# Page scores of a paged-attention decode step: five dimension steps in three runs instead of five single steps

## Chip, cores and metric

The kernel runs on one core of a Trainium2 chip. The metric is the device time of one execution in microseconds (us), lower is better. An execution consists of one program for five engines: TensorE (PE, matmuls and, as PEld, its weight loads), VectorE (DVE), ScalarE (ACT), GpSimd (POOL) and SyncE (SP, which only issues transfers here).

## The reference

One layer of a hybrid decoder is computed for a prompt of 1024 tokens and, with the same weights, for 8 sequences of 4 new tokens. The change concerns only the second attention branch of the 8 sequences. Each of them has 64 pages of 128 past tokens in a paged cache; each past token has a latent of 256 dimensions and a rotary key of 64. All 8 heads share these keys, and the latent is the value too:

```python
def one_seq(args):
    ql, qr, pt, c_new, r_new = args
    c_past = cache_ckv[pt].reshape(-1, KV_LORA)
    r_past = cache_kr[pt].reshape(-1, MLA_ROPE)
    s_past = jnp.einsum('thc,kc->htk', ql, c_past) + jnp.einsum('thr,kr->htk', qr, r_past)
    ...
    sc = jnp.concatenate([s_past.astype(jnp.float32) * scale, s_new], axis=-1)
    p = jax.nn.softmax(sc, axis=-1).astype(c_new.dtype)
    n_past = c_past.shape[0]
    return (jnp.einsum('htk,kc->thc', p[..., :n_past], c_past)
            + jnp.einsum('htk,kc->thc', p[..., n_past:], c_new))
```

So a score is a sum over 320 dimensions, in any order of the dimensions. The rest of the layer (projections of x, retention, prompt attention, down projections, output, norms) is not touched.

## The kernel before

The kernel goes through its stages in order: latents of all tokens, queries of the 8 sequences, page attention, retention of four heads, prompt attention of eight heads, down projections, output. In the early stages two streams are written out together: a main stream and a fill, the fill being the input projections `gate_tiles` whose results go to DRAM. Both are Python generators that yield an assumed cost. `beside(main, total, fill, budget)` draws from the fill whenever the fill's share of its budget lies behind the main stream's share of its total. For page attention this is `beside(page_attention(), 505, fill, 321)`: for each unit of cost that the main stream yields, 321/505 units of fill follow. One step of the fill (`mac` in `gemm`, lines 268 to 270) is three matmuls of 128x128 weights with 352 columns and yields 0.441. A third of a projection is eight such steps, ended by an evacuation on ACT (L441) and a store issued by ACT. The weights of the next projection are loaded by SP (L248) into two halves, turned into a high part on ACT (L249) and a low part on DVE (L200).

`page_attention` treats the 8 sequences in four groups `g` of two, and the 64 pages in four parts `jj`: 16 units. Before the first unit of a group, `new_tokens` scores the new tokens. A unit is `past_keys(g, jj, st)`:

- POOL gathers the rope keys (`rraw`, two rooms) and the latents (`craw`, four rooms: this unit's and the next one's) of both sequences with indirect DMAs (L631, L632).
- Five dimension steps, the rope's (j = 8) first, then j = 0, 2, 4, 6. A step turns 64 dimensions of both sequences with four DVE transposes (L691) into a room `kt`. There are two such rooms. Then it issues 16 matmuls (L695) on 32x32 tiles of PE's array, which add up in the four PSUM banks of `sc`. A matmul of 32-bit floats stands as two in the trace, so a step has 32 there.
- Softmax: ACT copies half of the sums out (L706), DVE adds the other half and takes the maximum (L707), ACT takes the exponentials (L711).
- PE transposes the probabilities (L720), ACT and DVE copy them out (L721), PE weights the latents with them on four column tiles (L726), DVE adds the result up (L728). L726 is the last reader of the unit's `craw` rooms.

A unit yields 5.0 behind the gathers, 2.5 between steps, 12.0 behind the softmax, 1.0 behind each half of the transposes and 1.0 at its end.

Within these streams, the order on each engine's queue is made by a planner. It takes the instructions as emitted unless it expects one not to be ready, in which case it puts a later one ahead. It also adds the waits and hands out the rooms: a room is given to the next tile once all readers of the last one are through.

## Time and profile before

| | us |
|---|---|
| median of 3 runs (2117.35 to 2122.88) | 2119.05 |
| span of the profiled execution | 2129.5 |
| PE busy in the span | 2079.5 |
| DVE, ACT, POOL busy | 1237.4, 692.8, 305.4 |
| page attention, about 185 to 725 us of the span: PE busy | 534.27 of 540 |
| the same stretch: DVE busy | 303.64 |

Busy time of PE is a union of matmuls that overlap in a pipeline and whose ends are modelled, so an engine that is busy all the time can still start matmuls closer together or farther apart; starts tell more than ends. In rows of the trace, "x32" is the number of instructions merged into one row, and what stands in brackets is the idle time before it and what ended it.

### The profile page before, as it was taken

How to read it: one execution, taken by the hardware profiler on the slowest of the kernel's cores; microseconds unless marked ns; L12 is line 12 of the kernel's file. 1: busy time of each engine (PE TensorE's matmuls, PEld its weight loads, DVE VectorE, ACT ScalarE, POOL GpSimd, SP SyncE). 2: the span in 40 equal slices, each digit the busy share in tenths (PEclk: the TensorE clock that was granted, in tenths of full speed). 3: DMA queues.
4: the chain of work that ended last, by engine and by line, in shares of the span. 5: the costliest groups of instructions: out<-in, count | busy, mean ns of one | idle time of the engine just before them, and what ended most of it. 6: DMA issues, size and time to landing. Idle time of an engine off the chain costs nothing. (4 is left out here: it accounts for less than half of the span.)

```text
span 2129.5 us, 38253 instructions
## 1 busy us (share of the span) xinstructions
PE 2079.5 (98%) x15122; PEld 1792.7 (84%) x15122; DVE 1237.4 (58%) x2699; ACT 692.8 (33%) x1455; POOL 305.4 (14%) x517
## 2 busy tenths in 40 slices
PE   8999999999999999999999999999999999999998
PEld 7898777777777897888878786788888999999976
DVE  6524555465655357667676663877777465454443
ACT  6312222433333222222222221454556232232221
POOL 2210110111110022222222120122211000000000
PEclk9999999999999999999999999999999999999999
DMA  7576656566565332554634746210112565236642
GB/s 211 129 241 211 234 186 237 187 244 216 211 228 178 111 94 51 175 163 120 204 67 151 191 134 221 64 49 18 38 52 92 187 217 173 89 122 132 172 153 91
DMA packets 387188, 321.90 MB, mean 151 GB/s; under 512 B 197984, under 2 KB 332320, under 8 KB 382912
## 3 DMA queue, kind: packets, MB, share of 16 engines
q1 hardware_dynamic: 290816, 205.86, 33.0%
q0 software_dynamic: 9216, 83.89, 10.5%
q10 hardware_dynamic: 86976, 29.70, 5.2%
q8 instruction: 119, 1.95, 0.4%
q14 instruction: 61, 0.50, 0.1%
HBM read 246.69 MB, written 72.69 MB: 150 GB/s over the span
## 5 line engine op out<-in xcount | busy, mean ns | idle before, releaser
L268 PE MATMUL mm<-xh,wh 128*128 128x352 f32 x1344 | 456.5, 340 | 4.8 <-ACT gev L441 3.2
L270 PE MATMUL mm<-xh,wl 128*128 128x352 f32 x1344 | 437.0, 325 | 2.1 <-DVE wl L200 2.1
L269 PE MATMUL mm<-xl,wh 128*128 128x352 f32 x1344 | 436.7, 325 | 0.0
L268 PEld LDWEIGHTS mm<-xh,wh 128*128 128x128 f32 x1344 | 253.7, 189 | 88.5 <-issue 76.8
L270 PEld LDWEIGHTS mm<-xh,wl 128*128 128x128 f32 x1344 | 254.6, 189 | 2.9 <-DVE wl L200 2.4
L269 PEld LDWEIGHTS mm<-xl,wh 128*128 128x128 f32 x1344 | 254.7, 189 | 2.5 <-issue 1.3
L691 DVE STREAM_TRANSPOSE kt<-craw 128x512 f32<-128x512 f32 x256 | 161.3, 681 | 108.8 <-PE sc L695 75.4
L200 DVE TENSOR_TENSOR wl<-wr,wh 128x512 fp32r<-128x512 f32 (+2 forms) x203 | 136.9, 686 | 98.7 <-ACT wh L249 69.1
L249 ACT CAST wh<-wr 128x512 fp32r<-128x512 f32 x150 | 89.8, 617 | 196.5 <-PE mm L269 169.8
L441 ACT ACTIVATE gev<-mm 128x352 f32<-128x352 f32 x120 | 55.5, 462 | 230.4 <-PE mm L270 221.8
L268 PE MATMUL mm<-mh,wh 128*128 128x352 f32 x384 | 124.8, 325 | 2.2 <-ACT mh L1210 0.8
L269 PE MATMUL mm<-ml,wh 128*128 128x352 f32 x384 | 124.7, 325 | 0.8 <-DVE ml L200 0.6
L270 PE MATMUL mm<-gh,wl 128*128 128x352 f32 x384 | 124.3, 324 | 0.0
L268 PE MATMUL mm<-gh,wh 128*128 128x352 f32 x384 | 124.3, 324 | 0.0
L270 PE MATMUL mm<-mh,wl 128*128 128x352 f32 x384 | 124.2, 324 | 0.0
L269 PE MATMUL mm<-gl,wh 128*128 128x352 f32 x384 | 124.1, 323 | 0.0
L268 PE MATMUL mm<-wv,xh 128*128 128x512 f32 x256 | 101.7, 397 | 0.0
L270 PE MATMUL mm<-wv,xl 128*128 128x512 f32 x256 | 100.9, 394 | 0.0
L269 PE MATMUL mm<-wv,xh 128*128 128x512 f32 x256 | 100.8, 394 | 0.0
L695 PE MATMUL sc<-kt,q 32*32 32x512 f32 x2560 | 91.2, 600 | 0.0
L268 PEld LDWEIGHTS mm<-mh,wh 128*128 128x128 f32 x384 | 72.4, 189 | 3.2 <-ACT gh L1210 1.2
L269 PEld LDWEIGHTS mm<-ml,wh 128*128 128x128 f32 x384 | 72.3, 188 | 1.6 <-DVE ml L200 1.4
(416 smaller groups left out, 4292.3 us busy)
## 6 DMA issues: line engine op xcount, KB each, us to landing
wr<-in_w_in_dram SPq DMA_DIRECT2D x144, 256.0 KB, 3.5
st<-in_state_ret_dram SPq DMA_DIRECT2D x32, 512.0 KB, 5.7
out_ret_sample_dram<-st SPq DMA_DIRECT2D x32, 512.0 KB, 3.1
gt<-gev ACTq DMA_DIRECT2D x48, 176.0 KB, 2.1
gl<-go SPq DMA_DIRECT2D x16, 528.0 KB, 5.1
rg<-gt SPq DMA_DIRECT2D x16, 528.0 KB, 4.2
gate<-ga SPq DMA_DIRECT2D x16, 528.0 KB, 3.6
wvS<-in_w_in_dram SPq DMA_DIRECT2D x32, 256.0 KB, 4.6
```

The lines of the kernel that those rows point to most:

```text
L200: dve.tensor_tensor(out=out, in0=src, in1=b32(hi), op=ALU.subtract)
L249: hi_by[0](hi, raw)
L268: pe.matmul(out, wh, xh, start=first, stop=False)
L269: pe.matmul(out, wh, xl, start=False, stop=False)
L270: pe.matmul(out, wl, xh, start=False, stop=last)
L441: a = act.activation(t, ps, func)
L691: dve.transpose(kt[:, 2 * i + s].rearrange("p (n r) -> p n r", r=32), src)
L695: pe.matmul(sc[32 * v:32 * v + 32, q, :], Q["q4"][qs_, j + v // 2, 2 * (g % 2) + v % 2, :], kt[qs_, v, :], start=n == 0, stop=n == NJ // 2 ...
```

## The change

The five steps of a unit are done in three runs: (j = 0 and 8), (4 and 2), (6). In a run all transposes are issued first, into both rooms, those of the second step of the run ahead of those of the first; then the matmuls of both steps follow with no yield between them. The accumulation starts at j = 0 and stops at j = 6. The yields of the unit are dealt anew: 1.0 behind the gathers (5.0 before), 8.4 behind the first run and 4.6 behind the second (four times 2.5 before), 13.0 behind the softmax (12.0 before). Their sum over a unit is 30.0 as before, and the arguments of `beside` stay.

```diff
-        yield 5.0
+        yield 1.0
         sc = psg.tile([P, 4, 512], F32, tag="sc", name="sc", bufs=1)
-        steps = [8, *range(0, 8, 2)]
-        for n, j in enumerate(steps):
-            kt = ring("kt")
-            for i in range(2):
-                for s in range(2):
-                    src = keys[s][:, :, 32 * (j + i):32 * (j + i) + 32] if j < 8 else rope[s][:, :, 32 * i:32 * i + 32]
-                    dve.transpose(kt[:, 2 * i + s].rearrange("p (n r) -> p n r", r=32), src)
-            for q in range(4):
-                qs_ = slice(32 * q, 32 * q + 32)
-                for v in range(4):
-                    pe.matmul(sc[32 * v:32 * v + 32, q, :], Q["q4"][qs_, j + v // 2, 2 * (g % 2) + v % 2, :], kt[qs_, v, :], start=n == 0,
-                              stop=n == NJ // 2 - 1, tile_position=(32 * q, 32 * v), skip_group_check=True)
-            if n + 1 < len(steps):
-                yield 2.5
+        runs = ((0, 8), (4, 2), (6,))
+        for n, js in enumerate(runs):
+            turned_keys = []
+            for j in reversed(js):
+                kt = ring("kt")
+                for i in range(2):
+                    for s in range(2):
+                        src = keys[s][:, :, 32 * (j + i):32 * (j + i) + 32] if j < 8 else rope[s][:, :, 32 * i:32 * i + 32]
+                        dve.transpose(kt[:, 2 * i + s].rearrange("p (n r) -> p n r", r=32), src)
+                turned_keys.insert(0, kt)
+            for j, kt in zip(js, turned_keys):
+                for q in range(4):
+                    qs_ = slice(32 * q, 32 * q + 32)
+                    for v in range(4):
+                        pe.matmul(sc[32 * v:32 * v + 32, q, :], Q["q4"][qs_, j + v // 2, 2 * (g % 2) + v % 2, :], kt[qs_, v, :], start=j == 0,
+                                  stop=j == 6, tile_position=(32 * q, 32 * v), skip_group_check=True)
+            if n < 2:
+                yield (8.4, 4.6)[n]
...
-        yield 12.0
+        yield 13.0
```

## Rows read from the trace of the kernel before

**Rows 1.** The page, first part: busy time, share of the span, instructions.

```profile
PE 2079.5 (98%) x15122; PEld 1792.7 (84%) x15122; DVE 1237.4 (58%) x2699; ACT 692.8 (33%) x1455; POOL 305.4 (14%) x517
```

**Rows 2.** Stretches: length, busy time of each engine, PE's clock, DMA share, GB/s.

```profile
185.00:725.00 540.00, 534.27 (x5897) 411.28 (x5896) 303.64 (x537) 177.21 (x289) 54.10 (x63) 1.00 0.58 203
```

**Rows 3.** Waits of PE, 185 to 725 us: total us, times, longest us.

```profile
PE x L720 <- ACT pr L711: 4.0, 9, 0.8
```

**Rows 4.** Groups by line, 185 to 725 us: busy us, mean ns, idle before.

```profile
L695 PE MATMUL sc<-kt,q 32*32 32x512 f32 x2560 | 91.2, 600 | 0.0
...
L200 DVE TENSOR_TENSOR wl<-wr,wh 128x512 fp32r<-128x512 f32 x60 | 39.9, 680 | 20.8 <-ACT wh L249 20.6
```

**Rows 5.** Timeline of PE, fourth unit: start us, duration us, engine, line, operation.

```profile
290.55 0.32 PE L270 MATMUL mm<-xh,wl 128*128 128x352 f32 x1
290.80 1.14 PE L695 MATMUL sc<-kt,q 32*32 32x512 f32 x32
291.87 0.43 PE L268 MATMUL mm<-xh,wh 128*128 128x352 f32 x1
292.14 0.32 PE L269 MATMUL mm<-xl,wh 128*128 128x352 f32 x1
...
294.01 1.14 PE L695 MATMUL sc<-kt,q 32*32 32x512 f32 x32
...
296.73 1.14 PE L695 MATMUL sc<-kt,q 32*32 32x512 f32 x32
```

**Rows 6.** Timeline: second half of a burst's matmuls; weight loads of a burst.

```profile
294.46 0.69 PE L695 MATMUL sc<-kt,q 32*32 32x512 f32 x16
...
299.93 0.23 PEld L695 LDWEIGHTS sc<-kt,q 32*32 32x32 f32 x32 [0.22 <-issue]
```

**Rows 7.** Timeline of PE at the end of the fourth unit.

```profile
313.22 3.66 PE L726 MATMUL x<-craw,pT 128*32 128x256 f32 x64 [0.92 <-DVE pT L721]
316.81 0.43 PE L268 MATMUL mm<-xh,wh 128*128 128x352 f32 x1
```

**Rows 8.** Timeline of DVE, fourth unit.

```profile
288.93 2.49 DVE L691 STREAM_TRANSPOSE kt<-craw 128x512 f32<-128x512 f32 x4 [4.78 <-PE sc L695]
292.13 1.90 DVE L691 STREAM_TRANSPOSE kt<-craw 128x512 f32<-128x512 f32 x3 [0.71 <-PE sc L695]
293.95 1.25 DVE L200 TENSOR_TENSOR wl<-wr,wh 128x512 fp32r<-128x512 f32 x2
295.12 3.08 DVE L691 STREAM_TRANSPOSE kt<-craw 128x512 f32<-128x512 f32 x5
...
303.11 1.31 DVE L691 STREAM_TRANSPOSE kt<-craw 128x512 f32<-128x512 f32 x2 [2.54 <-remote]
```

**Rows 9.** Timeline of POOL behind the fourth unit's end: gathers of latents.

```profile
317.17 0.94 POOL L632 DMA_INDIRECT craw<-in_cache_ckv_dram,idx  x1 [6.09 <-PE x L726]
318.42 0.93 POOL L632 DMA_INDIRECT craw<-in_cache_ckv_dram,idx  x1 [0.31 <-PE x L651]
```

**Rows 10.** Instructions on the tile of latents, 185 to 725 us: gathers' landing.

```profile
DMA to landing us min/median/max: 8.5/13.3/14.4
```

**Rows 11.** Timelines of DVE and PE at the first unit.

```profile
189.21 1.30 DVE L691 STREAM_TRANSPOSE kt<-craw 128x512 f32<-128x512 f32 x2 [4.28 <-DMA q4D<-sel]
...
191.01 1.30 DVE L691 STREAM_TRANSPOSE kt<-craw 128x512 f32<-128x512 f32 x2
...
191.07 1.14 PE L695 MATMUL sc<-kt,q 32*32 32x512 f32 x32
```

**Rows 12.** Timelines of ACT and POOL at the last bursts of units four and seven.

```profile
303.11 1.01 ACT L706 COPY sums<-sc 64x1024 f32<-64x1024 f32 x1 [3.09 <-remote]
...
405.85 1.01 ACT L706 COPY sums<-sc 64x1024 f32<-64x1024 f32 x1 [0.85 <-PE sc L695]
...
301.48 0.94 POOL L631 DMA_INDIRECT rraw<-in_cache_krope_dram,idx  x1 [0.31 <-issue]
...
405.90 1.12 POOL L631 DMA_INDIRECT rraw<-in_cache_krope_dram,idx  x1 [15.27 <-DVE kt L691]
```

## The prediction

> **What bounds the kernel now.** I read the page's first part, then the stretches by stage, then the groups of the stage that the change touches, then PE's timeline inside it. TensorE (PE) is busy for 98% of the span [rows 1], so time is gained only where PE does the same work in less time or waits less. [...]

> [...] A dimension step is one burst: 16 matmuls in the code, 32 in the trace, on 32x32 tiles of the array, two for each of 16 tiles. 2560 of them [rows 4] are 80 bursts: 16 units of 5. I read starts, because ends are modelled. Bursts with 12 projection matmuls between them start 3.21 us apart (290.80, 294.01), with 9 between them 2.72 us (294.01, 296.73) [rows 5]. Three matmuls more cost 0.48 to 0.49 us, so a projection matmul takes 0.1615 us and a burst takes 2.72 - 9 x 0.1615 = 1.267 us of PE. Of that, how much is scoring? The second half of the burst of 294.01 starts at 294.46 [rows 6]: a group of 16 matmuls streams in 0.45 us, a burst in 0.90 us. The other 0.367 us is the way in and out: the burst starts 0.25 us behind the last projection matmul, where 0.16 is normal, and the second projection matmul behind it starts 0.27 us after the first (291.87, 292.14) [rows 5]. 80 bursts pay this, 29 us in all.

> **The change part by part.** *Joined steps.* The five steps become runs of two, two and one. In a run the eight DVE transposes are issued first and the 32 matmuls of the code follow with no yield between. Each unit enters and leaves the tiled form 3 times instead of 5. If the second step of a run starts one group pitch behind the first, it costs 0.90 us instead of 1.267: 16 units x 2 joints x 0.367 = **-11.7 us**. The trace shows no two bursts together, so this is bounded from neighbours. The nearest row is the weighted sum over the values, L726: 64 matmuls on 4 column tiles, 16 groups with fresh weights each, 3.66 us less one duration of 0.38 over 15 pitches = 0.219 us for 256 columns [rows 7]. Twice that is 0.438 us for 512 columns, hence 0.876 us a step and -12.5 us. The other end: the weights of the second step's first group can't be loaded beforehand. The 32 loads of a burst take 0.23 us [rows 6]; exposed at each of 32 joints they cost 7.4 us and leave -4.3 us. I take -11.7, because L726 changes weights 15 times in a row with no sign of that.

> All matmuls, transposes, copies and gathers stay in number. The fill too: yields of a unit add up to 30.0 before (5.0, four of 2.5, 12.0, three of 1.0) and after (1.0, 8.4, 4.6, 13.0, three of 1.0). A yielded unit brings 321/505/0.441 = 1.441 projection steps of three matmuls.

> *Transposes of a run.* Both rooms of turned keys are filled for one run, so those of the next start only when the run has read them. Let run 1 start on PE at 0. Its matmuls end at 1.14 + 0.90 = 2.04; DVE starts 0.19 us later, as at 292.13 [rows 8] behind the burst of 290.80 to 291.94 [rows 5]; eight transposes at 2.49/4 = 0.623 us [rows 8] are done at 7.21. PE comes to run 2 after 2.167 us of run 1 and 12 steps (8.4 x 1.441), 36 x 0.1615 = 5.81: at 7.98. So 0.77 us to spare. Run 3: four transposes are done at 2.04 + 0.19 + 2.49 = 4.72, PE comes at 2.167 + 18 x 0.1615 = 5.07: 0.35 us to spare. Were a room given back after the first step of a run, both have 0.9 us more. What eats the margin is other DVE work in the queue: the low parts of the projection weights, L200, 60 of 0.68 us in the stage [rows 4], 3.75 in a unit, in pairs of 1.25 to 1.30 us. A pair inside run 2's filling costs 0.5 us, inside run 3's 0.95. Spread evenly, with 1.9 pairs in a unit's 33 us, 0.28 pairs fall into 5 us and 0.14 into 2.5 us: 16 x (0.28 x 0.5 + 0.14 x 0.95) = 4.4 us. But each engine's queue is put in order by readiness, not only as emitted: L200 stands amid transposes [rows 8], and DVE now has holes of 2 us behind each run in which L200 fits. So between 0 and 4.4, **+1 us**, nearer the end with the holes, as PE waited for no burst in before (0.0 us idle ahead of L695 [rows 4]).

> *Softmax.* From the last burst to L720 the fill grows from 12.0 to 13.0 yielded units, 1.4 steps or 0.70 us of PE. L720's nine waits are at most 0.8 us long, 4.0 us together [rows 3]. They nearly vanish: -4.0 to 0, **-3 us**. The cover has one new edge: the next unit's first keys, transposed ahead of the softmax's L707 in DVE's queue, need gathers that are issued 0.3 and 1.5 us behind L726's end, 316.88 [rows 7, 9], and land in 13.3 us, at most 14.4 [rows 10]: by 15.9 us. Behind L726 PE starts run 1 after 1.6 us (316.81 + 0.27 + 7 x 0.1615 + 0.25), so the last run ends after 1.6 + 7.98 + 5.07 + 1.14 = 15.8 us and DVE asks for those keys at 16.0: in time, with nothing left over. Before, by the same sum, the last burst ended after 17.5 us.

> *Between L726 and the first step* fill falls from 6.0 to 2.0 yielded units, 27 matmuls to 9. Both rooms were filled long before in all units but the first. There DVE starts the second room at 189.21 and ends it at 191.01 + 1.30 = 192.3, because the room was lent out for a store until then; PE started the first burst at 191.07 [rows 11] and would now come 18 x 0.1615 = 2.9 us sooner, at 188.2, needing both rooms. That is a wait of 4.1 us, or none if projections are put ahead: **+2 us**, once.

> *Queues.* POOL's rope gathers wait for the rope transposes, which stay the first in a unit; its key gathers wait for L726, not moved. ACT and SP keep their weight casts, evacuations and loads, tied to the fill, whose total is unchanged.

> Sum: -11.7 + 1 - 3 + 2 = **-11.7 us** on a span of 2129.5 us. The profiled execution is 10 us above the median of the timed runs (2119.05); a term of half a per cent carries over unchanged: 2107.4 us.

> **Rivals.**
> *The rooms come back late (slower).* At a unit's last burst, readers in 12 of 16 units start some 2 us late: in the fourth unit the last burst starts 3.20 us behind the burst of 296.73, at 299.93 [rows 5, 6], and ends at 301.07, but ACT's copy and a DVE transpose start at 303.11 [rows 8, 12], while POOL issues the next rope gathers until 302.42. In the seventh unit those gathers come later, at 405.90, and ACT's copy starts at 405.85, released by the burst itself [rows 12]. If such a delay of 2.04 us falls on the ends of runs 1 and 2, run 2 waits 1.08 us and run 3 1.50 us: 16 x 2.58 = 41 us, or 2149 us in all. It outweighs the gain from a delay of about 1.1 us in every unit. For it: key gathers are issued close by, from 0.3 us after L726 [rows 9]. Against: they end 2.5 us behind L726, and run 1 only at 3.6 us; and bursts one to four were answered after 0.2 us throughout. Chance 0.10.
> *The weights are not loaded ahead (no measurable change).* Were the loads of the second step held until the first step's matmuls are through, the joints give -4.3 instead of -11.7: 2114.8 us. Against it: a burst issues all its 32 loads within 0.23 us of its start [rows 6], while its first 16 matmuls stream for 0.45 us on the same tiles. [...] Chance 0.09.
> *The steps don't join.* If projections get between the steps of a run, all 80 bursts pay 1.267 us and only L720's waits and the new waits remain: about 2119 us. For it: queues are ordered by readiness. Against it: the room that is filled last is the one read first, so both are ready at once. Chance 0.08.

> **How the numbers follow.** Forecast 0.73, rivals 0.10, 0.09 and 0.08. The forecast's own range adds the good ends (-12.5 + 0 - 4 + 0 = -16.5) and, at the bad end, full L200 and first-unit terms with no L720 gain (-11.7 + 4.4 + 4.1 = -3.2): 2102.5 to 2116. For 8 in 10 I take 2101 to 2118, which leaves out the late rooms and part of the unjoined case. A measurement tells about 0.3% (6.4 us) from no change: faster means below 2112.7 us. Of the forecast's 0.73 some 0.03 lie above that; faster 0.70, same 0.20 (0.03, 0.09 and 0.08), slower 0.10.

> **What would show it.** Right: rows of L695 with 64 matmuls of about 2.04 us, three starts in a unit 8 and 5 us apart; the same busy clock; L720's waits near 0; the stage some 12 us shorter and all others alike. Joints wrong: third group later than 0.45 us behind the second. Waits wrong: PE waiting for L691, by 0.5 to 1.5 us at second and third runs. The prediction fails if DVE can't fill both rooms within 12 steps of projections, or if something in a later stage moves by more than 5 us.

## The result, and the profile after

| | before, us | after, us |
|---|---|---|
| median, side by side | 2120.55 | 2127.20 |
| ratio after/before | | 1.0030, interval 1.0022 to 1.0037 |
| profiled execution: its time, its span | span 2129.5 (first), 2119.1 (e1) | 2127.76, 2126.0 |
| page attention, start of the first L650 to start of the last L784 (after: L788) | 549.5 (first), 540.9 (e1) | 545.2 |

The change makes the kernel 0.3% slower, 6.6 us by the medians; 11.7 us less were forecast, and the range ended at 2118. One of the 20 executions of after, 3354 us at a granted clock of 0.556, stays out of the ratio. All lines of the changed part stand a few numbers later now: L691 is L693, L695 is L699, L707 L711, L711 L715, L720 L724, L726 L730.

One thing has to be settled before anything is compared. The profile of before that the prediction read (span 2129.5) is not typical for the executions of this result (2115.7 to 2126.1 us for before); the same kernel profiled again as e1 spans 2119.1 us. So after is held against e1 here, and the difference between the two profiles of before gets a place of its own (e12, e13).

The first line of after's page answers to [rows 1]. Behind it stand two stretches with the columns of [rows 2], from the stage's first L650 to its last L784 or L788: e1's, then after's.

```profile
PE 2078.7 (98%) x15122; PEld 1805.3 (85%) x15122; DVE 1235.0 (58%) x2699; ACT 696.5 (33%) x1457; POOL 306.6 (14%) x517
```

```profile
179.45:720.36 540.91, 540.91 (x5970) 421.03 (x5970) 307.25 (x550) 179.75 (x294) 54.13 (x63) 1.00 0.58 205
```

```profile
180.16:725.37 545.21, 542.89 (x5971) 433.49 (x5970) 305.35 (x550) 182.71 (x296) 54.52 (x63) 1.00 0.58 203
```

PE is as busy as in [rows 1]. Of the 6.9 us between the spans of after and e1, 4.3 lie in the stage, 2.3 of these as idle time of PE. Another 1.9 lie behind the stage, where after's granted clock is 0.50 for 3.4 us; e1 has no such stretch there, but e12, the kernel before, has one too, so it is not shown to belong to the change. The first line is after's, the second e12's (columns of [rows 2]):

```profile
725.70:729.10 3.40, 3.40 (x13) 3.40 (x13) 1.00 (x2) 0.00 (x0) 2.67 (x9) 0.50 0.59 166
```

```profile
730.00:733.40 3.40, 3.40 (x14) 3.40 (x13) 0.56 (x1) 0.00 (x0) 2.40 (x8) 0.51 0.72 216
```

The waits of PE in the stage of after (columns of [rows 3]) name the place, and the timeline of PE in the fourth unit shows what the joining did (columns of [rows 5]).

```profile
PE sc L699 <- DVE kt L693: 2.3, 1, 2.3
```

```profile
286.75 0.32 PE L270 MATMUL mm<-xh,wl 128*128 128x352 f32 x1
287.00 2.35 PE L699 MATMUL sc<-kt,q 32*32 32x512 f32 x64
289.27 0.43 PE L268 MATMUL mm<-xh,wh 128*128 128x352 f32 x1
289.54 0.32 PE L269 MATMUL mm<-xl,wh 128*128 128x352 f32 x1
...
295.29 2.35 PE L699 MATMUL sc<-kt,q 32*32 32x512 f32 x64
...
300.67 1.14 PE L699 MATMUL sc<-kt,q 32*32 32x512 f32 x32
```

The steps are joined: rows of 64 matmuls, three starts in a unit, 8.3 and 5.4 us apart. But a run of two costs 289.54 - 286.75 - 2 x 0.1615 = 2.47 us by the sum of the prediction, where 2.17 were forecast. A single burst still costs 1.267 us (16 of them in after, 80 in e1). The second step therefore costs 1.207 us instead of 0.90: joining saves 0.06 us a joint, not 0.367.

The weight loads of the same run tell where the 0.3 us go. This is the timeline of PE's loads in after, and below it the same from 287.995 us on, which splits the last row of 31 into its first load and the other 30:

```profile
286.99 0.23 PEld L699 LDWEIGHTS sc<-kt,q 32*32 32x32 f32 x32 [0.21 <-issue]
287.45 0.10 PEld L699 LDWEIGHTS sc<-kt,q 32*32 32x32 f32 x1 [0.23 <-issue]
287.88 0.55 PEld L699 LDWEIGHTS sc<-kt,q 32*32 32x32 f32 x31 [0.32 <-issue]
```

```profile
288.07 0.37 PEld L699 LDWEIGHTS sc<-kt,q 32*32 32x32 f32 x30
```

All 32 loads of the first step, two for each of its 16 matmuls, go within 0.23 us. When the second of a tile's two matmuls (its second pass) starts in the first step, at 0.45 us, one load of the second step follows: the first pass of the 17th matmul, whose second pass is loaded at 0.88 us. The 18th matmul's load and all behind it stand until 1.07 us. So the second step starts at about 1.08 us instead of 0.90.

The first unit is the other place. Timelines of DVE and PE there, and three stretches with the clock (columns of [rows 2]):

```profile
187.40 2.49 DVE L693 STREAM_TRANSPOSE kt<-craw 128x512 f32<-128x512 f32 x4 [4.85 <-DMA q4D<-sel]
```

```profile
185.53 0.32 PE L270 MATMUL mm<-xh,wl 128*128 128x352 f32 x1
188.16 5.51 PE L699 MATMUL sc<-kt,q 32*32 32x512 f32 x64 [2.32 <-DVE kt L693]
193.60 0.43 PE L268 MATMUL mm<-xh,wh 128*128 128x352 f32 x1
193.87 0.32 PE L269 MATMUL mm<-xl,wh 128*128 128x352 f32 x1
```

```profile
186.00:189.80 3.80, 1.64 (x5) 0.40 (x6) 2.40 (x4) 0.00 (x0) 0.00 (x0) 1.00 0.04 15
189.80:193.20 3.40, 3.40 (x60) 1.11 (x58) 2.37 (x5) 0.00 (x0) 0.00 (x0) 0.50 0.45 122
193.20:196.00 2.80, 2.80 (x28) 2.40 (x16) 2.80 (x6) 0.00 (x0) 0.00 (x0) 0.99 0.14 42
```

PE waits 2.32 us for the second room, starts on the first of its four transposes and has to follow the other three: DVE is through at 189.89. That makes 2.32 us ahead of the run and 1.73 us inside it, 4.05 us. By the sum used above the run costs 193.87 - 185.53 - 0.323 = 8.02 us, 5.5 more than others; the remaining 1.5 us are put down to the clock, whose granted rate falls to 0.50 for 3.4 us right behind this wait.

DVE, in the fourth unit of after, was never late:

```profile
288.32 4.86 DVE L693 STREAM_TRANSPOSE kt<-craw 128x512 f32<-128x512 f32 x8 [2.33 <-PE sc L699]
...
296.88 2.48 DVE L693 STREAM_TRANSPOSE kt<-craw 128x512 f32<-128x512 f32 x4
```

It starts 1.32 us behind the run of 287.00, that is, a room comes back after the run's first step. The eight transposes end at 293.18; PE wants them at 295.29. The third run's are done at 299.36, for 300.67.

### The profile page after: what moved, and what is told of

Its sections match the earlier page's. It is cut to its first block, busy times and chain, and to the rows that moved or that the text cites. A ratio compares the mean times of both kernels' runs of the same rounds, so it can differ in the third digit from the quotient of the medians.

```text
span 2126.0 us, 38247 instructions
## 1 busy us (share of the span) xinstructions
PE 2078.7 (98%) x15122; PEld 1805.3 (85%) x15122; DVE 1235.0 (58%) x2699; ACT 696.5 (33%) x1457; POOL 306.6 (14%) x517
## 4 chain that ended last, share of the span: by engine, by line
PE 86%; issue 4%; DMA 3%; DVE 3%; POOL 2%; ACT 2%; SPq 0%; POOLq 0%; ACTq 0%; DVEq 0%
PE mm L268 21%; PE mm L269 20%; PE mm L270 20%; PE sc L699 4%; PE x L730 3%; PE ac L269 2%; PE ac L268 2%; PE ac L270 2%; PE mm L1400 2%; DMA gl<-go 1%; PE tr L1386 1%; PE ac L1126 1%; PE ac L1343 1%; PE x L724 1%; PE ac L1347 1%
## 5 line engine op out<-in xcount | busy, mean ns | idle before, releaser
L693 DVE STREAM_TRANSPOSE kt<-craw 128x512 f32<-128x512 f32 x256 | 159.9, 680 | 85.0 <-PE sc L699 79.9
L200 DVE TENSOR_TENSOR wl<-wr,wh 128x512 fp32r<-128x512 f32 (+2 forms) x203 | 136.9, 687 | 97.9 <-ACT wh L249 69.1
L699 PE MATMUL sc<-kt,q 32*32 32x512 f32 x2560 | 97.6, 608 | 2.3 <-DVE kt L693 2.3
```

What stands on the lines that cost most here:

```text
L200: dve.tensor_tensor(out=out, in0=src, in1=b32(hi), op=ALU.subtract)
L693: dve.transpose(kt[:, 2 * i + s].rearrange("p (n r) -> p n r", r=32), src)
L699: pe.matmul(sc[32 * v:32 * v + 32, q, :], Q["q4"][qs_, j + v // 2, 2 * (g % 2) + v % 2, :], kt[qs_, v, :], start=j == 0, stop=j == 6, tile ...
```

## The experiments

Four groups of kernels ran, each group on one chip beside runs of the kernel before: e1 to e4 (before: 2121.11), e5 to e8 (2122.71), e9 to e11 (2130.40), e12 to e14 (2130.72). Ratios are against these; a difference in us that is told with a ratio is the ratio's, times that median.

### e1: the kernel before, again

No edit.

> The kernel before, unchanged. [...]

Measured: 2121.07, ratio 0.9995 (0.9985 to 1.0006), span 2119.1. No wait of PE stands in the stage, where [rows 3] had 4.0 us at L720. The profile that the prediction rests on had 10 us that this one has not, in the same program.

### e2: the first unit's run put off

```diff
-        yield 1.0
+        yield 8.0 if g == 0 and jj == 0 else 1.0
...
-    beside(page_attention(), 505, fill, 321)
+    beside(page_attention(), 512, fill, 325.45)
```

> The changed kernel, with 8.0 instead of 1.0 yielded ahead of the first run of the first unit only (and total and budget of the fill raised in proportion, 512 and 325.45). Theory 'the first unit's wait is the loss': PE's waits for the second room there (2.3 us ahead of the run and 3.2 us inside it in the changed kernel) and the 3.4 us at the lower clock level behind them vanish: 5.5 to 7.2 us less than the changed kernel, ratio to before 0.999 to 1.001. Rival 'the loss lies elsewhere': within 2 us of the changed kernel, ratio 1.002 to 1.004.

Measured: 2119.58, ratio 0.9986 (0.9976 to 0.9997), 3.0 us below before. The first run now starts at 192.47 and lasts 2.35 us as all others; PE has no wait in the stage, and the stretch at a granted clock of 0.50 at the first unit is gone (1.00 from 182 to 200 us). What is left of the change is then a small gain. All 32 runs of two cost 2.474 us (79.1 in all), the 16 single steps 1.267 (20.3): 99.4 us against 101.3 in e1, 1.9 us less.

### e3: rows and columns of tiles exchanged in a burst

```diff
-                for q in range(4):
-                    qs_ = slice(32 * q, 32 * q + 32)
-                    for v in range(4):
+                for v in range(4):
+                    for q in range(4):
+                        qs_ = slice(32 * q, 32 * q + 32)
```

> The changed kernel with the two loops over tiles exchanged, so that consecutive matmuls of a step take different row groups of the array. In the changed kernel the second step of a run costs 1.20 us, 0.30 us more than two group pitches: the matmuls of its first group start at 0.88 and then 1.07 to 1.30 us of the run instead of 0.88 to 0.98. Theory 'loads wait for matmuls in their own row group': here loads can go ahead into other row groups, a run of two takes 2.05 us instead of 2.35 in the trace and the kernel gains about 0.3 x 32 = 9.6 us on the changed kernel. Rival 'any second step on the same 16 tiles pays it': 2.35 us again, time as the changed kernel within 2 us.

Measured: 2124.21, ratio 1.0017 (1.0006 to 1.0028). A run costs 2.47 us as before and its loads come in the same pattern, one ahead and the rest from 1.07 us. Whether neighbours in the queue are on the same row group of the array makes no difference here, 2.47 us either way, so waiting for matmuls in their own row group is not what holds the loads.

### e4: only the softmax's fill

```diff
-        yield 5.0
+        yield 4.0
...
-        yield 12.0
+        yield 13.0
```

(in the kernel before)

> The kernel before with one yielded unit moved from ahead of the first step (5.0 to 4.0) to behind the softmax (12.0 to 13.0), five single steps kept. Theory 'more fill hides PE's waits ahead of L720': these fall from 4.0 to under 1 us in the trace and the time falls by 2 to 4 us, ratio 0.998 to 0.999. Rival 'these waits move elsewhere': ratio 1.000 or above.

Measured: 2122.61, ratio 1.0006 (0.9995 to 1.0017): nothing, as there was no wait at L720 on this chip to take away.

### e5: the first room released at the end of a run

The order in a run is tiles 0 to 14 of the first step, 0 to 14 of the second, then tile 15 of both (on top of e2).

```diff
+            order = [(j, kt, t // 4, t % 4) for ts in (range(15), range(15, 16)) for j, kt in steps for t in ts]
+            for j, kt, q, v in order:
```

> The kernel of e2_first_unit, with the order of the 32 matmuls of a joined run changed in one place: the matmul of the first step's last tile stands behind the other 15 matmuls of the second step, and the second step's last tile ends the run. Nothing is left out. The last reader of the first room of turned keys, whose end tells DVE that the room is free, thereby moves from the middle of the run to its end. Theory R (what holds the second step's weight loads is that matmul with its report to DVE in the middle of the run: in the changed kernel only one load goes ahead, and the next comes 1.07 us behind the run's start, about when the report is sent): the second step starts 0.43 us behind the second half of the first, a run of two costs about 2.17 us instead of 2.47, and 32 runs bring 9.6 us: about 2110 us against 2119.6 in e2, less what DVE loses by getting the first room 0.9 us later (0 to 4 us). Theory T (a second step on the same 16 tiles waits until the array has drained, whoever is told of it): the third group of 16 matmuls still starts about 1.07 us behind the first, a run costs 2.4 to 2.5 us, the time stays at 2119 to 2121 us.

Measured: 2146.03, ratio 1.0116 (1.0100 to 1.0132), and a run costs 3.31 us. The loads of one run:

```profile
329.04 0.23 PEld L699 LDWEIGHTS sc<-kt,q 32*32 32x32 f32 x30 [0.22 <-issue]
329.50 0.11 PEld L699 LDWEIGHTS sc<-kt,q 32*32 32x32 f32 x2 [0.23 <-issue]
329.93 0.54 PEld L699 LDWEIGHTS sc<-kt,q 32*32 32x32 f32 x30 [0.32 <-issue]
330.79 0.10 PEld L699 LDWEIGHTS sc<-kt,q 32*32 32x32 f32 x1 [0.32 <-issue]
331.22 0.10 PEld L699 LDWEIGHTS sc<-kt,q 32*32 32x32 f32 x1 [0.32 <-issue]
```

Theory R (the report in the middle of the run holds the loads) falls: with no report there, the loads still stop. But the number is telling. Now two loads of the second step go ahead where one did. In after, 16 + 1 matmuls of the code had a load in; here 15 + 2. The sum is 17 both times. The extra 0.84 us is tile 15: both its steps are now at the end, one behind the other, alone on the array.

### e6: a run cut in the middle

As e5, with `(range(8), range(8, 16))`.

> As e5, but the run is cut in the middle: tiles 0 to 7 of the first step, tiles 0 to 7 of the second, tiles 8 to 15 of the first, tiles 8 to 15 of the second. Nothing is left out. Theory R: the report stands behind the 24th matmul, and only what comes after it can be held: the run costs 2.2 to 2.35 us, the time is 2110 to 2116 us. Theory T, taken by tiles (a tile's second step needs the array drained of the group ahead of it): there are now two reuses in a run instead of one, but each has eight tiles streaming beside it; the run costs 2.5 us or more, the time is 2119 to 2128 us.

Measured: 2142.89, ratio 1.0093 (1.0079 to 1.0107), 3.20 us a run. Loads of the run of 332.01, in windows one behind the other:

```profile
332.01 0.23 PEld L699 LDWEIGHTS sc<-kt,q 32*32 32x32 f32 x17 [0.22 <-issue]
```

```profile
332.47 0.13 PEld L699 LDWEIGHTS sc<-kt,q 32*32 32x32 f32 x5 [0.23 <-issue]
```

```profile
333.09 0.23 PEld L699 LDWEIGHTS sc<-kt,q 32*32 32x32 f32 x15
```

The second row begins the second step of tiles 0 to 7: eight loads 7 ns apart from 0.46 us on (the window cuts the row at five), as soon as each tile's first step is in its second half. So a second step on the same tiles does not have to wait for anything to drain: theory T falls. And of the first row's 17 loads 16 are the two passes of tiles 0 to 7; the last one is tile 8 of the first step, the 17th matmul of the code. The 18th matmul is tile 9, which is idle and fresh, and it gets its load at 333.09 only (third row), 1.08 us behind the run's start. What is counted are matmuls, not tiles. This is **theory W**: PE takes in 17 matmuls of the code, and the next one only when the oldest is finished. The oldest starts its second pass at 0.45 us and that lasts 0.59 us in the trace (ends are modelled), so it is finished at 1.04; the 18th matmul's load comes at 1.07 in after, at 1.08 here.

A matmul of the code stands as two matmuls and two loads in these traces, so what is counted may also be these instructions. No run separates the two, as all have matmuls of two passes. Matmuls streaming in the same rows did not hold these loads: in e6 eight loads go, from 0.46 us on, to tiles whose own rows are streaming, and e3 shows no effect of the rows' order.

### e7: the first unit alone

The kernel before, with `runs`, yields and order of the changed kernel where `g == 0 and jj == 0`.

The diff is against the changed kernel.

```diff
+        first = g == 0 and jj == 0
+        yield 1.0 if first else 5.0
...
+        runs = ((0, 8), (4, 2), (6,)) if first else ((8,), (0,), (2,), (4,), (6,))
...
+        yield 13.0 if first else 12.0
```

> The kernel before, with the first of the 16 units alone done as in the changed kernel (runs of two, two and one, yields 1.0, 8.4, 4.6, 13.0) and the other 15 as before. Nothing is left out. [...]

Measured: 2128.19, ratio 1.0028 (1.0017 to 1.0040): 5.9 us slower from one unit of 16, so the loss is not spread over the later units. PE's row of that unit's first run, and the stretch from 186.80 on:

```profile
186.41 5.81 PE L700 MATMUL sc<-kt,q 32*32 32x512 f32 x64 [2.02 <-DVE kt L694]
```

```profile
186.80:193.60 6.80, 6.80 (x69) 3.20 (x68) 5.77 (x11) 0.00 (x0) 0.00 (x0) 0.50 0.29 78
```

The first run costs 8.22 us, 5.75 more than a run of two, and the granted clock is 0.50 for 6.8 us from 186.80 on, projections included. With e2 this is shown from both sides: take the first unit's wait away and the loss goes; put it alone into the kernel before and the loss comes.

### e8: both steps of a tile side by side

As e5, with `order = [(j, kt, t // 4, t % 4) for t in range(16) for j, kt in steps]`.

> The kernel of e2_first_unit, with the two steps of a run interleaved tile by tile: both steps' matmuls of a tile stand next to each other. Nothing is left out. Theory R: the report comes with the 31st matmul, so it holds nothing, but the second matmul on a tile has to wait for the first one. If the array's 16 tiles are served independently of each other, the run costs 2.1 to 2.2 us and the time is 2109 to 2113 us; if a matmul that waits holds those behind it, the tiles are served one after the other and the run costs at least 16 x 0.45 = 7 us more, 2350 us or so. Theory T: 2.47 us or more, 2119 us or more.

Measured: 2175.69, ratio 1.0246 (1.0230 to 1.0261), 4.15 us a run: not 2.1 to 2.2 as with independent tiles, nor 7 us more as with tiles one after the other. W explains it. 17 open matmuls are eight tiles with both their steps and one more; tiles 9 to 15 stand idle. Loads of one run:

```profile
337.94 0.23 PEld L699 LDWEIGHTS sc<-kt,q 32*32 32x32 f32 x17 [0.22 <-issue]
338.40 0.72 PEld L699 LDWEIGHTS sc<-kt,q 32*32 32x32 f32 x18 [0.23 <-issue]
339.45 0.10 PEld L699 LDWEIGHTS sc<-kt,q 32*32 32x32 f32 x1 [0.33 <-issue]
339.88 1.19 PEld L699 LDWEIGHTS sc<-kt,q 32*32 32x32 f32 x28 [0.33 <-issue]
```

The first three rows are 36 loads, nine tiles with two steps of two passes. Tile 9, the 19th matmul, opens the last row, 1.94 us behind the start. The second matmul of the code, tile 0's second step, starts its second pass at 1.31 us and is finished 0.59 later, at 1.90.

### e9 and e10: theory W on single bursts of short matmuls

The kernel before, each matmul cut into two of 256 columns; e9 has both halves of a tile side by side, e10 first all first halves. Neither computes the reference's scores; the number of bursts and columns stays. Each ran once.

```diff
-            for q in range(4):
-                ...
-                for v in range(4):
+            for q, v, h in [(t // 4, t % 4, h) for t in range(16) for h in range(2)]:
+                hs_ = slice(256 * h, 256 * h + 256)
```

(e10: `for h in range(2) for t in range(16)`)

> The kernel before, with each matmul of a dimension step cut into two of 256 columns, both halves of a tile next to each other: a single burst now has 32 matmuls in the code, on the same 16 tiles, with the same columns in all. Nothing is left out and no steps are joined. Theory W (formed on e5 to e8): TensorE takes in no more than 17 matmuls of the code ahead of the oldest unfinished one; the 18th load comes when the first matmul is finished, 1.07 us behind its start with 512 columns, and one follows every 16.7 ns from there. With 256 columns a group pitch is 0.22 to 0.24 us and a matmul lasts about 0.38 us, as in L726 of before, so the first one is finished at about 0.65 us: the 18th load comes there and not at 1.07; tiles 9 to 15 start no matmul before that although they are idle, and a burst costs 1.9 to 2.45 us instead of 1.27, in all 50 to 95 us more than before, 2170 to 2215 us. Rival U (tiles are served independently and nothing counts matmuls): a burst costs 1.27 to 1.35 us, the time is 2120 to 2127 us.

> As e9, but the first half of the columns on all 16 tiles, then the second half on all 16. Nothing is left out. Theory W: the 17th matmul (tile 0 again) starts after two group pitches at 0.46 us, the 18th load comes at about 0.65 us, the last load 14 x 16.7 ns later at 0.88, and its second pass ends at about 1.32 us instead of 0.98: a burst costs about 1.6 us, 80 of them 27 us more, 2147 us. Rival D (a fixed delay of 1.07 us from a burst's start, whatever the size of a matmul): the 18th load at 1.07 us, a burst costs about 2.0 us, 2180 us. Rival U: 1.27 to 1.35 us, 2120 to 2127 us.

Measured: a burst costs 2.45 us in e9 and 1.62 us in e10 (medians of 80), where W had 1.9 to 2.45 and about 1.6, and independent tiles 1.27 to 1.35. The first row below is PE in e10, the other two its loads:

```profile
342.27 1.50 PE L695 MATMUL sc<-kt,q 32*32 32x256 f32 x64
```

```profile
342.40 0.44 PEld L695 LDWEIGHTS sc<-kt,q 32*32 32x32 f32 x3
```

```profile
342.92 0.36 PEld L695 LDWEIGHTS sc<-kt,q 32*32 32x32 f32 x30
```

The 18th matmul's load opens the third row, 0.65 us behind the burst's start, as forecast, and not 1.07 (the three loads of the second row end those of the first 17): the hold lasts as long as the oldest matmul does, and rival D falls. In e9, whose burst of the same kind starts at 355.95, tiles 9 to 15 are idle until this row of its loads, 1.08 us behind the start:

```profile
357.03 0.76 PEld L695 LDWEIGHTS sc<-kt,q 32*32 32x32 f32 x28
```

The times are 2252.4 and 2183.6 us, 122 and 53 above before, where W's sums were 50 to 95 and 27. At these medians the bursts make 80 x 1.18 = 94 us and 80 x 0.35 = 28 us. The rest is not spread over them. In e9 14 bursts cost 4.1 to 5.2 us and in e10 13 cost 3.5 to 3.9: just those beside which POOL issues both rope gathers. By the starts they add 27 us in either run, and 94 + 27 and 28 + 27 are what was measured. One such burst of e10, its loads, and POOL:

```profile
201.80 3.57 PE L695 MATMUL sc<-kt,q 32*32 32x256 f32 x64
```

```profile
201.79 0.86 PEld L695 LDWEIGHTS sc<-kt,q 32*32 32x32 f32 x46 [0.23 <-DVE kt L691]
203.21 0.15 PEld L695 LDWEIGHTS sc<-kt,q 32*32 32x32 f32 x5 [0.55 <-issue]
203.95 0.16 PEld L695 LDWEIGHTS sc<-kt,q 32*32 32x32 f32 x6 [0.59 <-issue]
```

```profile
201.94 0.94 POOL L631 DMA_INDIRECT rraw<-in_cache_krope_dram,idx  x1 [31.12 <-DVE kt L691]
203.18 0.94 POOL L631 DMA_INDIRECT rraw<-in_cache_krope_dram,idx  x1 [0.30 <-issue]
```

The loads come in small groups with holes that no engine's report explains. Single bursts of 16 matmuls do not show this: in e12 all 80 cost 1.267 us, with gathers beside them too. The granted clock falls as well, to a mean of 0.98 in the stage of e9 and 0.99 in e10; by the starts that costs the projections 10 and 6 us, about as much as the waits at L720 that e12 has and these two have not (7 and 6 us).

### e11: the changed kernel, again

No edit to the changed kernel.

> The changed kernel itself once more, to add its single causes up. From e2 to e8: joined steps 32 x 0.06 = -1.9 us, the first unit's wait and the clock behind it +5.9 us (e7). If these are all: +4 us, a ratio of 1.0019, 2125 us beside 2121. If something else in the later units costs too: 1.003 or more, over 2127 us.

Measured: 2132.19 beside 2130.40, ratio 1.0008 (0.9998 to 1.0018): less than the causes found so far add up to, and on a chip where before takes 9 us longer. So something costs before more there than after (e12 to e14). After pays something of its own there, too: 11 of its 32 runs of two cost 2.75 to 3.27 us, 3.8 us over 2.474 in all. They are just the runs beside which POOL issues a gather of latents. In the profile of after the same 11 runs have their gathers beside them and cost 2.47, one of them 2.57. PE and POOL in e11, then POOL in after, beside its run of 287.00:

```profile
290.42 2.64 PE L699 MATMUL sc<-kt,q 32*32 32x512 f32 x64
```

```profile
290.37 0.94 POOL L632 DMA_INDIRECT craw<-in_cache_ckv_dram,idx  x1 [0.30 <-issue]
```

```profile
286.95 0.94 POOL L632 DMA_INDIRECT craw<-in_cache_ckv_dram,idx  x1 [0.31 <-issue]
```

### e12, e13, e14: the waits at L720

e12 is the kernel before, e13 the edit of e4, e14 that of e2.

> The kernel before, unchanged, for its profile. If L720's waits come with executions that take longer: near 2130 us and a span near 2128 the profile shows 3 to 4 us of waits at L720, near 2121 us it shows none. If they come and go by chance, they may stand in a profile of 2119 us too.

> The kernel before, with 1.0 more of yield behind the softmax and 1.0 less behind the gathers, as in e4; nothing else. Where the profile of e12 shows L720's waits: 3 to 4 us faster than before. Where it shows none: no difference (within 2 us), as in e4.

> As e2: the changed kernel with the first unit's first run put off. 32 joined steps save 0.06 us each: 1.9 us faster than before where e12 shows no waits at L720 (e2 had 3.0, with an interval from 0.5 to 5.1), and about 5 us where it does.

Measured: e12 2129.24, ratio 0.9990 (0.9976 to 1.0004); e13 2125.76, ratio 0.9982 (0.9970 to 0.9994); e14 2124.81, ratio 0.9971 (0.9958 to 0.9984). PE's waits at L720 in e12, then in e13:

```profile
PE x L720 <- ACT pr L711: 3.9, 8, 0.8
```

```profile
PE x L720 <- ACT pr L711: 0.2, 1, 0.2
```

The waits of [rows 3] are there again, together with a time of 2129 us, and the later softmax takes them: 3.8 us faster (1.3 to 6.4). On e4's chip the same edit did nothing. e14 is 6.2 us faster (3.4 to 8.9); this version was faster than before on both chips on which it ran.

The waits understate what L720 costs, as they count idle time alone. By the starts, the places from the last projection to L720, from one L720 to the next, and from the last projection to L726 take 26.6 us in e12 and 19.6 in e1: 7.0 us, nearly all of the 8 by which e12's stage is longer. They take 22.1 us in e13, 21.1 in e11 and 21.0 in e14. e14 also has 11 runs of two beside gathers that cost more, as e11 has, 4.2 us in all.

Where the waits come from shows in ACT's copy out of the last burst, in the fourth unit. In e1, the timelines of PE, ACT and POOL:

```profile
295.87 1.14 PE L695 MATMUL sc<-kt,q 32*32 32x512 f32 x32
```

```profile
297.20 1.01 ACT L706 COPY sums<-sc 64x1024 f32<-64x1024 f32 x1 [1.24 <-PE sc L695]
```

```profile
297.43 0.94 POOL L631 DMA_INDIRECT rraw<-in_cache_krope_dram,idx  x1 [0.30 <-issue]
```

There ACT starts 1.33 us behind the burst's start, before POOL issues its second gather. In the first profile of before the copy starts 3.18 us behind a burst's start, after POOL's issue [rows 6, 12], and in e12 likewise (297.68 and 300.84):

```profile
300.84 1.01 ACT L706 COPY sums<-sc 64x1024 f32<-64x1024 f32 x1 [3.08 <-remote]
```

The program is the same in both. In e1, e2, e5, e7 and after the copy starts at most 1.0 us behind the start of the burst's last matmul, with one unit at 1.3; in the first profile of before and in e11 to e14 it is 2.3 us or more in 11 to 14 of the 16 units. In e10, on e11's chip, 13 units have their gathers issued before the burst ends and ACT's copy starts at most 0.8 us behind the last matmul's start; in the one unit whose gathers come at the end it is 2.98. So the late readers go together with the gathers, in these executions alone. Why they are late was not found, nor whether the chip decides: the first profile of before spans 2129.5 us beside timed runs of 2117 to 2123.

## Why the prediction was wrong

**What bounds the kernel.** Right: PE, without cover. Every term below went straight into the time.

**Joined steps, -11.7 us: the step that failed.** Way in and out were rightly priced at 0.367 us a burst, and 32 of them are gone. What failed is "if the second step of a run starts one group pitch behind the first, it costs 0.90 us". It costs 1.207, as by theory W the 18th matmul waits until the first is finished (its load comes at 1.07 us in after and e6, at 0.65 in e10), so the term is -1.9 us. The evidence for 0.90 was the burst itself, whose 32 loads go ahead [rows 6], and L726 [rows 7]. Both stay below 17: a burst is 16 matmuls of the code, and L726 has only 4 tiles: a matmul of 256 columns is open for about 0.60 us (0.22 + 0.38 [rows 7]) and four start every 0.44 us, so that, by this estimate, five or six are open. Nothing in the stage of before was found to ask for more than 17, and the bound of -4.3 us for the bad end was too good as well, since it priced the loads and not the wait for the oldest matmul.

**The rivals.** "The weights are not loaded ahead" saw the place and a third group later than 0.45 us, but with another mechanism and too small a price (2114.8). "The rooms come back late" did not come: rooms come back after a run's first step, in after 1.32 us behind its start and in e11, in the fourth unit, 1.62. What the gathers beside a run did hold in e11 and e14 were PE's own matmuls, which no rival named. "The steps don't join" did not come either.

**Transposes, +1 us (0 to 4.4).** 0: no wait for L693 outside the first unit, so L200 cost nothing.

**First unit, +2 us (0 to 4.1).** The wait came in full, about 4.05 us, because nothing was put ahead of it. Taking the mean of "4.1 or none" was no estimate of either case. And a piece was missing altogether: the granted clock fell to 0.50 behind the wait, so the unit costs 5.9 us (e7).

**Softmax, -3 us (-4 to 0).** Right on one chip (3.8 us, e13), nothing on another (e4). The row [rows 3] was true, though idle time alone understates what these places cost (7.0 us by the starts in e12), but it belonged to an execution of 2129.5 us beside a median of 2119. The prediction said that "a term of half a per cent carries over unchanged"; a wait of 4 us is the very kind of thing by which two executions 10 us apart differ.

**The sum.** On the chips of the result -1.9 + 5.9 + 0 = +4.0 us by the parts, against +6.4 measured (4.7 to 7.8); e7's own interval is 3.6 to 8.5, so the two can be reconciled, but up to 2.4 us have no cause shown. Where L720 waits, and with e12 taken for before: -1.9 + 5.9 - 5.6 at L720 and L726 + 3.8 for the runs beside gathers = +2.2 us, against +1.7 (-0.4 to 3.8) in e11. Without the first unit, -1.9 against -3.0 (-5.1 to -0.6) in e2, and -1.9 - 5.7 + 4.2 = -3.4 against -6.2 (-8.9 to -3.4) in e14, where the sum lies at the edge of the interval.

## What to carry to other kernels

Before short operations are put together, ask how many the engine holds open at once, and look in the trace for a place with as many as the new one will have; a smooth short burst says nothing about one twice as long. When a stage is moved forward, price its first round by itself: a cover that is there in 15 rounds and missing in the first cost more here than all joints brought. And read a wait from more than one execution before it is put into a sum, above all if the profiled time lies away from the median.
